# The last unit of an RWKV time-mixing kernel: both V projections ahead of the previous unit's output matmuls, copies and stores shared out anew

## The chip, the cores and the metric

The kernel runs on one core of a Trainium2 chip. The metric is the device time of one launch in microseconds (us); less is better. The kernel before takes 204.8 us (median of 5 runs, 204.01 to 205.72).

The engines are called PE (TensorE, matrix multiplies; PEld is its weight loading), DVE (VectorE), ACT (ScalarE), POOL (GpSimd) and SP (SyncE). SP does no arithmetic here: it issues DMAs. A DMA is issued by an instruction in the stream of SP, ACT or POOL, and 16 DMA engines then move its packets. Matrix products are written to PSUM; from there ACT or DVE copies them to on-chip memory (SBUF), and a DMA stores them to the output in device memory (HBM).

## The reference

`x` has shape (16, 2048, 256) in float32, and `x_prev` is `x` shifted by one row along the sequence.

```
xv = x * time_mix_v + x_prev * (1 - time_mix_v)
xr = x * time_mix_r + x_prev * (1 - time_mix_r)
v = xv @ value_weight
r = xr @ receptance_weight
out = (sigmoid(r) * v) @ output_weight        # float32, (16, 2048, 256)
```

The key projection is computed by the reference, but its result is not used, and the kernel leaves it out.

## The kernel before, in words

The 32,768 rows are worked in 64 **units** of 512 rows, numbered 0 to 63; four units make one batch. For each unit the kernel transposes its rows (by PE in the early batches, by DMA in the last four), mixes them with the previous rows, and then does, in bf16:

- R, the receptance projection (`project(..., 0)`, line 275, matmuls at L279) into PSUM, and a sigmoid on ACT (L513) into `s_sb`;
- V, the value projection (L279), and on DVE the product `z = s * v` (L548) into `z_sb`;
- O, the output projection (`out_matmuls`, line 301, matmuls at L303), a copy of the result from PSUM into `o_sb` in float32, and a store.

The order on every engine is the order in which the Python code records the instructions (`tc.manual_schedule()`); there is no planner. The framework adds the semaphore waits that the data and the reuse of buffers ask for. PSUM is full: `ps_t` has two buffers of one bank, and `ps_v`, `ps_r` and `ps_o` have one buffer of two banks each. A tile that is taken again from a pool of one buffer waits until its last reader is done.

The steady loop (lines 500 to 561) runs units 0 to 62. In the last rounds O of unit g-1 is recorded after V of unit g. From unit 60 on, `output` (line 323) does O in two halves of 256 rows by `out_part` (line 315): the matmuls, one copy, one store each. The stores before the last unit are all issued by SP.

The last unit, 63, is written out by hand in `last_unit` (line 347). It works in halves and quarters so that the end of the pipeline is short:

- line 358: R of half 0 into `psum_r` and its sigmoid (L360), R of half 1 into a `ps_t` buffer and its sigmoid;
- `value(h)` (line 361): V of half h, into `psum_v` for h = 0 and into the other `ps_t` buffer for h = 1, and the product z on DVE (L364);
- `before(h)` (line 368): half h of O of unit 62, whose z is `z_prev`: four matmuls (L303) into `psum_o` for h = 0 or `psum_r` for h = 1, a copy (L320) and a 256 KB store (L313);
- four quarters of O of unit 63 (lines 376 to 379): two matmuls each, into `psum_v`, `psum_o` and the two `ps_t` buffers; a 128x256 copy; a 128 KB store each.

In what follows, V63a and V63b are the two halves of V of unit 63, z63a and z63b their products on DVE, O62a and O62b the two halves of O of unit 62, and O63-0 to O63-3 the four quarters of O of unit 63. S62a, S62b and S63-0 to S63-3 are the stores of these six results, 1 MB together.

At the very end SP executes nine waits, one after the other, each on two semaphores: the lanes that count the landing of the DMAs. The framework deals each DMA one of 8 hardware lanes (SP and ACT) or one of 8 software lanes (POOL) and writes the nine waits in a fixed order. A barrier of all engines follows.

Of the kernel before, what the change touches and what calls it, by code (L numbers as in the profile page):

```python
# [15 lines left out]
def kernel(  # L16
# [25 lines left out]
    nc = tc.nc  # L42
# [11 lines left out]
    H = UJ // 2  # L54
# [16 lines left out]
    ps_t_pool = ctx.enter_context(tc.tile_pool(name="ps_t", bufs=2, space=bass.MemoryType.PSUM))  # L71
    ps_v_pool = ctx.enter_context(tc.tile_pool(name="ps_v", bufs=1, space=bass.MemoryType.PSUM))
    ps_r_pool = ctx.enter_context(tc.tile_pool(name="ps_r", bufs=1, space=bass.MemoryType.PSUM))
    ps_o_pool = ctx.enter_context(tc.tile_pool(name="ps_o", bufs=1, space=bass.MemoryType.PSUM))
# [200 lines left out]
    def project(ps, g, m, lo=0, hi=TU):  # L275
        b, e = divmod(g, UB)
        for mo in range(KO):
            for ko in range(KO):
                nc.tensor.matmul(  # L279
                    out=ps[:, mo, :],  # L280
                    lhsT=w_bf[:, m, ko, mo * P : (mo + 1) * P],
                    rhs=mixed((b, m, e * TU + lo, e * TU + hi))[:, :, ko],
                    start=(ko == 0),
                    stop=(ko == KO - 1),
                )
# [15 lines left out]
    def out_matmuls(ps, z, jj, slot):  # L301
        for ko in range(KO):
            nc.tensor.matmul(  # L303
                out=ps[:, slot, :],
                lhsT=z[:, ko, jj * P : (jj + 1) * P],
                rhs=wo_bf[:, ko, :],
                start=(ko == 0),
                stop=(ko == KO - 1),
            )

    def store(queue, b, lo, hi):
        dst = out[b].rearrange("(p j) d -> p j d", p=P)
        queue.dma_start(out=dst[:, lo:hi, :], in_=o_sb[b][:, lo:hi, :])  # L313

    def out_part(pool, name, z, b, e, jj, n, copy, queue):
        ps = pool.tile([P, n, D], FP32, name=name)
        for k in range(n):
            out_matmuls(ps, z, jj + k, k)
        lo = e * UJ + jj
        copy(out=o_sb[b][:, lo : lo + n, :], in_=ps)  # L320
        store(queue, b, lo, lo + n)
# [25 lines left out]
    def last_unit(g):  # L347


        b, e = divmod(g, UB)  # L350
        s_sb = zpool.tile([P, KO, TU], BF16, name="s_sb")
        z_sb = zpool.tile([P, KO, TU], BF16, name="z_sb")
        cols = [(h * H * P, (h + 1) * H * P) for h in range(2)]
        spare = [(ps_r_pool, "psum_r"), (ps_t_pool, "ps_t"), (ps_v_pool, "psum_v"), (ps_t_pool, "ps_t")]
        banks = [pool.tile([P, KO, H * P], FP32, name=name) for pool, name in spare]

        by_act, by_dve = nc.scalar.copy, nc.vector.tensor_copy
        for h, (lo, hi) in enumerate(cols):
            project(banks[h], g, 0, lo, hi)
            nc.scalar.activation(out=s_sb[:, :, lo:hi], in_=banks[h], func=ACT.Sigmoid)  # L360
        def value(h):
            lo, hi = cols[h]
            project(banks[2 + h], g, 1, lo, hi)
            nc.vector.tensor_tensor(  # L364
                out=z_sb[:, :, lo:hi], in0=s_sb[:, :, lo:hi], in1=banks[2 + h], op=ALU.mult
            )

        def before(h):
            pool, name = [(ps_o_pool, "psum_o"), (ps_r_pool, "psum_r")][h]
            out_part(pool, name, z_prev, b, e - 1, h * H, H, by_act, nc.sync)  # L370

        before(0)
        value(0)
        before(1)
        value(1)
        out_part(ps_v_pool, "psum_v", z_sb, b, e, 0, 1, by_act, nc.sync)
        out_part(ps_o_pool, "psum_o", z_sb, b, e, 1, 1, by_dve, nc.sync)
        out_part(ps_t_pool, "ps_t", z_sb, b, e, 2, 1, by_act, nc.scalar)
        out_part(ps_t_pool, "ps_t", z_sb, b, e, 3, 1, by_dve, nc.sync)

    def tile_for(b):

# [80 lines left out]
    by_act = {g: [] for g in range(-1, NU)}  # L463
# [36 lines left out]
    for g in range(NU - 1):  # L500
# [46 lines left out]
        z_sb = zpool.tile([P, KO, TU], BF16, name="z_sb")  # L547
# [9 lines left out]
        if shifted is not None and g == max(UB * (shifted - 2), CROSS + 2):  # L557
            nc.sync.dma_start(
                out=xt[shifted][:, 0, :, 1:P], in_=xt[shifted][:, J, :, 0 : P - 1]
            )  # L560
        z_prev2, z_prev = z_prev, z_sb
    last_unit(NU - 1)


# [28 lines left out]
```

## Time and profile before

| quantity | value |
|---|---|
| median of 5 runs | 204.8 us |
| the profiled execution, its own time | 205.07 us |
| its span, first to last instruction | 203.1 us |
| granted PE clock | 1.00 |
| busy share: PE / DVE / ACT / POOL | 97% / 92% / 88% / 41% |
| DMA, mean over the span | 281 GB/s |
| last matmul of O62b / of O63-3 ends | 197.55 us / 199.45 us |
| last copy (S63-3's data) ends | 199.90 us |
| last store issued by SP | 199.93 us |

The span is 1.9 us shorter than the execution's own time; what lies around it belongs to starting and ending a launch. Over the whole kernel PE is the busy engine. The change touches only what happens after about 196 us, where PE runs out of work, so the end has to be read by itself: on a timeline of the last 8 us, which gives for each instruction its start, its length and the wait before it, and in windows that show how much of the time the 16 DMA engines were busy.

### The profile page before, as it was taken

To read this page: it belongs to the slowest core of one execution; us is meant where nothing else is said; L and a number is where in the kernel's file an instruction comes from. 1 tells how busy PE (TensorE), PEld (TensorE's weight loads), DVE (VectorE), ACT (ScalarE), POOL (GpSimd) and SP (SyncE) were. 2 spreads that over 40 slices of the span, in tenths; PEclk is the share of its full clock that TensorE was granted. 3 is DMA by queue.
4 is the path that set the end of the run, shared out by engine and by line. 5 is a ranking of instruction groups with operands and counts; after the bars stand their busy time and mean duration, and the time that the engine had idled before them with its cause. 6 is when DMAs were issued, how large, how long until landed. Compare 5 with 4: busy or idle time off the path is not lost.

```text
span 203.1 us, 3923 instructions
## 1 busy us (share of the span) xinstructions
PE 196.6 (97%) x1436; PEld 127.4 (63%) x1436; DVE 186.7 (92%) x301; ACT 179.3 (88%) x198; POOL 83.3 (41%) x109
## 2 busy tenths in 40 slices
PE   7999999999999999999999999999999999999992
PEld 6766566666666666666666666656565656665571
DVE  3589999999999999999999999999999999999962
ACT  2399999999999999999999999998899999999981
POOL 1744462354344625426443444423444444444200
PEclk9999999999999999999999999999999999999999
DMA  4999999999999999999999999989999999999475
GB/s 164 295 155 216 215 280 275 277 282 271 290 315 307 319 309 300 311 305 289 296 294 290 312 302 290 323 292 205 295 175 359 249 341 254 259 418 377 203 305 207
DMA packets 32186, 57.00 MB, mean 281 GB/s; under 512 B 20772, under 2 KB 22056, under 8 KB 29096
## 3 DMA queue, kind: packets, MB, share of 16 engines
q1 hardware_dynamic: 27216, 40.50, 59.1%
q0 software_dynamic: 4800, 16.12, 40.0%
q8 instruction: 11, 0.18, 0.3%
q10 hardware_dynamic: 152, 0.13, 0.2%
q14 instruction: 7, 0.06, 0.1%
HBM read 34.34 MB, written 33.55 MB: 334 GB/s over the span
## 4 chain that ended last, share of the span: by engine, by line
PE 87%; ACT 4%; DVE 2%; issue 2%; DMA 2%; SPq 0%; DVEq 0%; ACTq 0%
PE psum_v L279 25%; PE psum_o L303 25%; PE psum_r L279 25%; PE ps_t L200 9%; DMA o_sb<-in_x_dram 2%; ACT s_sb L513 2%; PE psum_r L293 1%; ACT o_sb L335 1%; DVE mix L271 1%; DVE z_sb L548 1%; PE psum_v L223 1%; PE ps_t L144 1%; PE ps_t L303 1%; DVE mix L249 1%; ACT mix L491 1%
## 5 line engine op out<-in xcount | busy, mean ns | idle before, releaser
L259 POOL TENSOR_SCALAR mix<-xt,c_sb 128x1024 bf16<-128x1024 bf16 (+1 forms) x55 | 61.0, 1109 | 91.6 <-DVE mix L271 83.8
L548 DVE TENSOR_TENSOR z_sb<-s_sb,psum_v 128x1024 bf16<-128x1024 bf16 x63 | 76.7, 1217 | 3.4 <-PE psum_v L279 1.7
L271 DVE TENSOR_TENSOR mix<-mix,xt 128x1024 bf16<-128x1024 bf16 x112 | 77.2, 697 | 1.7
L279 PEld LDWEIGHTS <-w_bf 128*128 128x128 bf16 x516 | 48.6, 98 | 38.5 <-issue 1.1
L513 ACT ACTIVATE s_sb<-psum_r 128x1024 bf16<-128x1024 f32 x63 | 65.0, 1032 | 5.1 <-PE psum_r L279 4.8
L335 ACT COPY o_sb<-psum_o 128x1024 f32<-128x1024 f32 x60 | 61.1, 1018 | 7.1 <-PE psum_o L303 7.1
L279 PE MATMUL psum_v<-mix,w_bf 128*128 128x512 bf16 (+1 forms) x256 | 65.3, 378 | 0.4 <-DVE z_sb L548 0.2
L279 PE MATMUL psum_r<-mix,w_bf 128*128 128x512 bf16 (+1 forms) x252 | 64.3, 378 | 0.3 <-ACT s_sb L513 0.3
L303 PE MATMUL psum_o<-wo_bf,z_sb 128*128 128x256 bf16 x494 | 64.4, 273 | 0.1
L303 PEld LDWEIGHTS <-z_sb 128*128 128x128 bf16 x512 | 49.9, 98 | 20.1 <-DVE z_sb L364 0.8
L216 ACT COPY xt<-ps_t 128x1024 bf16<-128x1024 bf16 x38 | 38.7, 1029 | 0.0
L200 PEld LDWEIGHTS <-x_bf 128*128 128x128 bf16 x344 | 22.6, 98 | 9.2
L200 PE MATMUL ps_t<-ident,x_bf 128*128 128x128 bf16 x344 | 25.8, 219 | 0.0
L249 DVE TENSOR_SCALAR mix<-xt,c_sb 128x1024 bf16<-128x1024 bf16 (+1 forms) x50 | 22.5, 459 | 0.0
L491 ACT ACTIVATE mix<-xt,c_sb 128x1024 bf16<-128x1024 bf16 x11 | 12.8, 1159 | 0.0
L109 POOL DMA_DIRECT2D x_bf<-in_x_dram x14 | 10.5, 753 | 0.0
L271 DVE TENSOR_TENSOR mix<-mix,xt_first 128x1024 bf16<-128x1024 bf16 x15 | 10.2, 685 | 0.1
L259 POOL TENSOR_SCALAR mix<-xt_first,c_sb 128x512 bf16<-128x512 bf16 x6 | 4.1, 685 | 9.6 <-DVE xt_first L408 8.0
L249 DVE TENSOR_SCALAR mix<-xt_first,c_sb 128x512 bf16<-128x512 bf16 x22 | 6.8, 358 | 0.3
L216 ACT COPY xt_first<-ps_t 128x1024 bf16<-128x1024 bf16 x5 | 5.2, 1034 | 0.0
L144 PE MATMUL ps_t<-zeros 128*128 128x128 bf16 x31 | 3.7, 313 | 1.0 <-DVE zeros L87 1.0
L209 ACT CAST xt_first<-ps_t 128x512 bf16<-128x512 f32 x4 | 2.1, 588 | 2.3 <-PE ps_t L200 2.3
(63 smaller groups left out, 49.1 us busy)
## 6 DMA issues: line engine op xcount, KB each, us to landing
out_dram<-o_sb SPq DMA_DIRECT2D x28, 1024.0 KB, 9.8
x_bf<-in_x_dram POOLq DMA_DIRECT2D x14, 1024.0 KB, 25.3
out_dram<-o_sb SPq DMA_DIRECT2D x4, 512.0 KB, 3.7
out_dram<-o_sb SPq DMA_DIRECT2D x6, 256.0 KB, 2.1
x_bf<-in_x_dram POOLq DMA_DIRECT2D x5, 256.0 KB, 7.2
o_sb<-in_x_dram SPq DMA_DIRECT2D x2, 512.0 KB, 4.9
o_sb<-in_x_dram SPq DMA_DIRECT2D x2, 256.0 KB, 3.4
out_dram<-o_sb SPq DMA_DIRECT2D x3, 128.0 KB, 1.9
```

The costliest lines, as they stand in the source:

```text
L109: return nc.gpsimd.dma_start(out=x_bf[b], in_=rows(b), max_dma_last_dim=8192)
L200: nc.tensor.transpose(out=ps[:, jj], in_=src[:, jj, ko * P : (ko + 1) * P], identity=idn)
L216: nc.scalar.copy(out=xt[b][:, j0 : j0 + UJ], in_=ps)
L249: nc.vector.tensor_scalar(out=mixed(piece)[:, :, ko], in0=xt[b][:, slots(piece), ko], scalar1=c_sb[:, m, ko : ko + 1], scalar2=None, op0=A ...
L259: op = nc.gpsimd.tensor_scalar(out=mixed(piece)[:, :, 1], in0=xt[b][:, slots(piece), 1], scalar1=c_sb[:, m, 1:2], scalar2=1.0, op0=ALU.mul ...
L271: return nc.vector.tensor_tensor(out=mixed(piece), in0=mixed(piece), in1=xt[b][:, slots(piece, 1)], op=ALU.add)
L279: nc.tensor.matmul(out=ps[:, mo, :], lhsT=w_bf[:, m, ko, mo * P : (mo + 1) * P], rhs=mixed((b, m, e * TU + lo, e * TU + hi))[:, :, ko], st ...
L303: nc.tensor.matmul(out=ps[:, slot, :], lhsT=z[:, ko, jj * P : (jj + 1) * P], rhs=wo_bf[:, ko, :], start=(ko == 0), stop=(ko == KO - 1),)
L335: nc.scalar.copy(out=o_sb[b][:, j0 : j0 + UJ, :], in_=ps)
L491: nc.scalar.activation(out=mixed(piece)[:, :, ko], in_=xt[b][:, slots(piece), ko], func=ACT.Copy, scale=c_sb[:, m, ko : ko + 1],)
L513: nc.scalar.activation(out=s_sb, in_=ps_r, func=ACT.Sigmoid)
L548: nc.vector.tensor_tensor(out=z_sb, in0=s_sb, in1=ps_v, op=ALU.mult)
```

## The change

Only `last_unit` changes. The two halves of V of unit 63 are recorded ahead of both halves of O of unit 62; before, they alternated, O62a, V63a, O62b, V63b. The copy of O62b goes from ACT to DVE and its store from SP's queue to POOL's. The quarters of unit 63 exchange their copying engines and queues:

| result | copied by, before | after | stored by, before | after |
|---|---|---|---|---|
| O62a | ACT | ACT | SP | SP |
| O62b | ACT | DVE | SP | POOL |
| O63-0 | ACT | ACT | SP | SP |
| O63-1 | DVE | ACT | SP | SP |
| O63-2 | ACT | DVE | ACT | SP |
| O63-3 | DVE | ACT | SP | ACT |

No matmul, copy or byte is added or taken away, and PSUM buffers stay as they were.

```diff
         def before(h):
             pool, name = [(ps_o_pool, "psum_o"), (ps_r_pool, "psum_r")][h]
-            out_part(pool, name, z_prev, b, e - 1, h * H, H, by_act, nc.sync)
-
+            copy, queue = [(by_act, nc.sync), (by_dve, nc.gpsimd)][h]
+            out_part(pool, name, z_prev, b, e - 1, h * H, H, copy, queue)
+
+        value(0)
+        value(1)
         before(0)
-        value(0)
         before(1)
-        value(1)
         out_part(ps_v_pool, "psum_v", z_sb, b, e, 0, 1, by_act, nc.sync)
-        out_part(ps_o_pool, "psum_o", z_sb, b, e, 1, 1, by_dve, nc.sync)
-        out_part(ps_t_pool, "ps_t", z_sb, b, e, 2, 1, by_act, nc.scalar)
-        out_part(ps_t_pool, "ps_t", z_sb, b, e, 3, 1, by_dve, nc.sync)
+        out_part(ps_o_pool, "psum_o", z_sb, b, e, 1, 1, by_act, nc.sync)
+        out_part(ps_t_pool, "ps_t", z_sb, b, e, 2, 1, by_dve, nc.sync)
+        out_part(ps_t_pool, "ps_t", z_sb, b, e, 3, 1, by_act, nc.scalar)
```

In the built program the six stores of units 62 and 63 are waited for by SP's nine last waits in these places: before, S63-2 in the third, S63-3 in the fourth; after, S62b (POOL's lane) and S63-2 in the third, S63-3 in the ninth.

## The prediction

> **What bounds the kernel now.** The page's chain of waits is 87% PE over the whole span, but the change acts only after 196 us, so I read the end in four views: the timeline, the DMA windows, the transfer rows, and the waits that close the program.
>
> The timeline (start, length, what ran, wait before it and its releaser) gives the chain of the last copies:
>
> ```profile
> 196.08 0.60 PE L303 MATMUL psum_o<-wo_bf,z_sb 128*128 128x256 bf16 x4
> 196.51 0.60 PE L279 MATMUL psum_v<-mix,w_bf 128*128 128x256 bf16 x4
> 196.88 0.62 ACT L320 COPY o_sb<-psum_o 128x512 f32<-128x512 f32 x1
> ...
> 197.22 0.69 DVE L364 TENSOR_TENSOR z_sb<-s_sb,psum_v 128x512 bf16<-128x512 bf16 x1 [1.29 <-PE psum_v L279]
> ...
> 198.09 0.69 DVE L364 TENSOR_TENSOR z_sb<-s_sb,ps_t 128x512 bf16<-128x512 bf16 x1 [0.18 <-PE ps_t L279]
> ...
> 198.70 0.42 DVE L320 COPY o_sb<-psum_o 128x256 f32<-128x256 f32 x1
> ...
> 198.84 0.61 PE L303 MATMUL ps_t<-wo_bf,z_sb 128*128 128x256 bf16 x4 [0.26 <-DVE z_sb L364]
> 199.26 0.37 ACT L320 COPY o_sb<-ps_t 128x256 f32<-128x256 f32 x1 [0.50 <-PE ps_t L303]
> 199.48 0.42 DVE L320 COPY o_sb<-ps_t 128x256 f32<-128x256 f32 x1 [0.37 <-PE ps_t L303]
> ```
>
> V63b ends late, z63b follows at 198.09, and PE stands until 198.84 for the last two quarters. This wait is what the change attacks. But the windows tell of a second bound. Columns: window, length, five engines' busy time, clock, busy share of the 16 DMA engines, GB/s:
>
> ```profile
> 197.90:198.35 0.45, 0.45 (x5) 0.31 (x4) 0.27 (x2) 0.27 (x1) 0.00 (x0) 1.00 0.00 0
> 198.36:201.31 2.95, 0.82 (x6) 0.31 (x4) 1.18 (x3) 0.74 (x2) 0.00 (x0) 1.00 0.97 349
> 201.47:203.10 1.63, 0.00 (x0) 0.00 (x0) 0.00 (x0) 0.00 (x0) 0.00 (x0) 1.00 0.00 0
> ```
>
> The DMA engines are idle until 198.36, then 97% busy for 2.95 us with the 1 MB of the six last stores. The first to be issued is S62a, by SP at 197.52; its packets move 0.84 us later. So the end is set by when this stretch starts and how long 1 MB takes, more than by the last copy. The last store, issued at 199.93, moves its last packet at 201.47.
>
> Then SP's closing waits (their number, lengths in ns, starts):
>
> ```profile
> L588 SPq EVENT_SEMAPHORE  x1: 28/28/28, 201.6 to 201.6; - x1
> ...
> L588 SPq EVENT_SEMAPHORE  x2: 27/28/28, 201.9 to 202.0; - x2
> ```
>
> The wait for S63-3, fourth of nine, ends at 201.94; five more follow 0.06 us apart, then a barrier, and the span ends at 203.15, 1.21 us after that wait.
>
> **The change, part by part.** Times are after's, worked out from before's rows. Four matmuls take 0.44 us from start to start; a copy or product starts 0.70 us after the first of the four matmuls it reads (V63a at 196.51, z63a at 197.22), 0.43 us after the first of two (O63-0 at 197.96, its copy at 198.39).
>
> *V63a and V63b first.* V63a starts at 196.08 instead of 196.51, V63b at 196.51 instead of 197.38. `psum_v` must be free of the product of unit 62 (L548, 194.71 + 1.22 = 195.93): it is, by 0.15 us, so this wait costs nothing; were the product later, PE and all behind it would be late by the excess. z63a runs at 196.78, and z63b, no longer waiting for PE but for DVE itself (0.61 us from one product to the next), at 197.40 to 198.08. Gain: z63b 0.69 us earlier.
>
> *O62a and O62b later.* O62a starts at 196.95 (+0.87), O62b at 197.38 (+0.43). O62a's copy on ACT runs 197.58 to 198.20 instead of to 197.50, so S62a is issued at 198.23 instead of 197.52: **+0.71 us**. Nothing hides it: the DMA engines are idle by then.
>
> *Added wait.* O63-1 reuses `psum_o` and must wait for that copy: ready at 198.04 after O63-0 at 197.82, it starts at 198.25, so 0.21 us lost. Behind it on PE stand O63-2 and O63-3, at 198.47 and 198.69 instead of 198.84 and 199.06.
>
> *Copies.* The 128x512 DVE copy of O62b has no row. 0.42 us for 256 columns and 0.69 for a product of 512 give 0.69; one that costs ACT's 0.59 or twice the 256 row, 0.84, bounds it. It runs 198.02 to 198.71, before O63-2 is ready at 198.89, so even 0.84 is hidden. The others: ACT O63-0 198.24 to 198.61, ACT O63-1 198.67 to 199.04, DVE O63-2 198.89 to 199.31, ACT O63-3 199.11 to 199.48.
>
> *Stores issued*, before and after: S62a 197.52, 198.23; S62b 198.19, 198.74 (POOL); S63-0 198.79, 198.64; S63-1 199.22, 199.07; S63-2 199.67, 199.44 (SP is free of S63-1 only at 199.40); S63-3 199.93, 199.52. The last issue comes **0.42 us earlier**. Taken alone, that is the gain.
>
> *The DMA engines.* The same 1 MB now starts at 198.23 + 0.84 = 199.07, not 198.36. No store is ready before S62a, and all but POOL's are ready when the one ahead ends: a 256 KB store occupies the engines for some 0.7 us, a 128 KB one for some 0.4 (2 x 0.7 + 4 x 0.4 = 3.0, the stretch). So the stretch ends 0.71 us later, less at most the 3% that it stood idle before (0.09): **+0.62 to +0.71 us**. The 0.42 us is swallowed.
>
> *POOL's store.* POOL has been idle since 190.6 and holds only the end behind it. The trace has no store from POOL. Its nearest row is a 256 KB load: issued at 6.75, no software packet before 8.4, landed 5.3 us after issue beside other loads. At 198.74 that gives first packets at 200.4. The SP and ACT stores need 0.7 + 4 x 0.4 = 2.3 us, to 201.4, so POOL's packets fall into a full stretch and need not lengthen it: I take 0. Below: if POOL's packets moved beside the others, 0.67 us would leave the stretch. Above: if it landed 5.3 us after issue, at 204.0, the waits and barrier would end near 205.3, 1.5 us above the forecast.
>
> The Trainium skill ("DMA: Bandwidth & Descriptors", section "Issuing engines are not separate DMA queues") speaks against the sharing out: all issuers end in the same 16 engines, and several issuers save only issue time. No row here shows a store from POOL next to SP's; by that rule the lower bound falls away and the stretch stays full. The same page ("Latency and other measured facts") gives about 0.6 us to the first byte for SP and ACT and 1 us for POOL; the trace has 0.84 and 1.7, and by the page's difference of 0.4 S62b would still fall inside the stretch, so the sum would stay.
>
> *Closing waits.* The store that ends the stretch is then S62b or S63-2, both in the third wait, one place earlier than S63-3 before: one more wait after it, +0.06. Should S63-3, now in the ninth, land last, five fewer follow: -0.30.
>
> **Sum**: +0.62 to +0.71, and +0.06: about **+0.7 us** on the profiled span, 203.15 to 203.85; +0.3 if S63-3 lands last. The profiled execution took 205.07, 0.27 above the median; I put the difference on the median: 204.8 + 0.7 = **205.5**, in itself 205.0 to 205.8. That is +0.34%, within 0.5%, about what a measurement of this kernel can tell from no change (1.02 us).
>
> **Rivals.**
>
> *A, the forecast*, the full DMA stretch starts later: 205.5. For it: 97%, and zero before it. Chance 0.62.
>
> *B, POOL's store is the last to land: slower.* Place: S62b, third wait. It decides as soon as POOL's packets come after 201.4, 2.6 us after issue, or take longer. Price: over the page's queue rows POOL's queue needs 40.0% of the engines for 16.12 MB, SP's 59.1% for 40.50, so 1.7 times the time for a written byte; 0.7 us becomes 1.2, on top of A +0.5: 206.0. By the 5.3 us row 207.0. For it: no packet of POOL's first load for 1.7 us. Against: those loads change the type, reading two bytes for each written, and were beside other loads. Chance 0.26, taken at 206.3.
>
> *C, the chain of copies sets the end: faster.* If the DMA engines take three queues at a higher rate than one, or the stretch still has slack, the 0.42 us comes through, with the ninth wait -0.72 in all: 204.1 to 204.8, taken at 204.4. Against: 349 GB/s at 97%. Chance 0.12.
>
> That the order isn't as written is excluded: the built program has it. The one step that could undo it is the wait on `psum_v`, with 0.15 us to spare.
>
> **Numbers.** The likeliest is A, 205.5. The range reaches down to C's middle, 204.4, and up to 206.6, B's first price and some half of its way to the second; some 0.06 and 0.10 lie outside. Faster by over 0.5% (below 203.8) needs more than C's far end: 0.03. Slower (above 205.8): all of B and a little of A, 0.30. Within: 0.67.
>
> **What would show it.** In the profile after: z63b near 197.4; S62a issued near 198.2 and the DMA engines idle from 197.9 to about 199.1; then a stretch of some 3 us at 95% or more; last copy near 199.5, earlier than before, and yet a later end. B shows as software packets after 201.4, C as a stretch well under 2.8 us or with idle time in it. I am wrong if S62a moves less than 0.4 us, or if 1 MB takes less than 2.5 us.

## The result and the profile after

The changed kernel takes 205.35 us (median of 54 runs), the kernel before 204.48 us (median of 94 runs beside them). The ratio is 1.004, 95% interval 1.0028 to 1.0052: slower by about 0.8 us, or 0.4%. The profiled execution took 205.54 us with a span of 203.6 us.

Up to unit 63 both programs are the same, yet its first R matmul started at 195.19 us in the profile before and at 194.89 after. In all the profiles below that start lies between 193.8 and 195.8, so spans and single times scatter by more than the effect. The measure used from here on is the **tail**, from that matmul to the end of the span, worked out from the trace: 7.96 us before, 8.74 after, **+0.78**. One kernel profiled twice (the sixth experiment) gave tails of 7.65 and 7.66. Subtract 0.30 from a predicted time to find it in this timeline of after (start, length, engine, line, what):

```profile
195.76 0.60 PE L279 MATMUL psum_v<-mix,w_bf 128*128 128x256 bf16 x4
...
196.64 0.60 PE L303 MATMUL psum_o<-wo_bf,z_sb 128*128 128x256 bf16 x4
...
197.07 0.68 DVE L364 TENSOR_TENSOR z_sb<-s_sb,ps_t 128x512 bf16<-128x512 bf16 x1
197.27 0.59 ACT L320 COPY o_sb<-psum_o 128x512 f32<-128x512 f32 x1 [0.56 <-PE psum_o L303]
...
197.71 0.69 DVE L320 COPY o_sb<-psum_r 128x512 f32<-128x512 f32 x1
197.91 0.38 PE L303 MATMUL psum_o<-wo_bf,z_sb 128*128 128x256 bf16 x2
...
198.13 0.60 PE L303 MATMUL ps_t<-wo_bf,z_sb 128*128 128x256 bf16 x4
...
198.54 0.42 DVE L320 COPY o_sb<-ps_t 128x256 f32<-128x256 f32 x1
198.70 0.61 POOL L313 DMA_DIRECT2D out_dram<-o_sb  x1 [8.45 <-DVE o_sb L320]
198.76 0.37 ACT L320 COPY o_sb<-ps_t 128x256 f32<-128x256 f32 x1
199.16 0.40 ACTq L313 DMA_DIRECT2D out_dram<-o_sb  x1
```

PE no longer waits for z63b (197.07 to 197.75; the quarters that need it start at 198.13), and the last copies end near 199.1, relative to the start of unit 63 about half a microsecond earlier than before. But O62a's copy, 197.27, is later, and S62a is issued only at 197.89. The DMA windows show what that does (length, engines' busy time, clock, DMA share, GB/s):

```profile
197.62:198.71 1.09, 1.07 (x9) 0.58 (x6) 0.95 (x3) 0.98 (x3) 0.01 (x1) 1.00 0.00 0
...
198.72:201.89 3.17, 0.01 (x1) 0.00 (x0) 0.25 (x1) 0.37 (x1) 0.59 (x1) 1.00 0.92 331
```

In the kernel before the idle time ahead of the last stores was 0.45 us; now it is 1.1. The stretch itself, first packet to last, is hardly longer: the same window of before is

```profile
198.36:201.47 3.11, 0.82 (x6) 0.31 (x4) 1.18 (x3) 0.74 (x2) 0.00 (x0) 1.00 0.93 337
```

So the 1 MB was moved nearly as fast as before (331 against 337 GB/s, 0.05 us more), and began 0.66 us later. The transfer rows of after, for two stores issued between 198.6 and 199.2 (last column: us from issue to landing), show the stores queueing. ACT's 128 KB store took 3.1 us:

```profile
out_dram<-o_sb POOLq DMA_DIRECT2D x1, 256.0 KB, 3.1
out_dram<-o_sb ACTq DMA_DIRECT2D x1, 128.0 KB, 3.1
```

ACT's 128 KB store of before took 1.9:

```profile
out_dram<-o_sb ACTq DMA_DIRECT2D x1, 128.0 KB, 1.9
```

SP's closing waits of after, from the third on:

```profile
L589 SPq EVENT_SEMAPHORE  x7: 28/28/28, 202.4 to 202.8; - x7
```

The third of nine ends at 202.4 with the landing of S63-2; the other six follow at 0.06 us each.

### The profile page after: what moved, and what is told of

Same layout as the page of the kernel before. It is cut to its first block, busy times and chain, and to the rows that moved or that the text cites. A ratio compares the mean times of both kernels' runs of the same rounds, so it can differ in the third digit from the quotient of the medians.

```text
span 203.6 us, 3922 instructions
## 1 busy us (share of the span) xinstructions
PE 195.9 (96%) x1436; PEld 127.4 (63%) x1436; DVE 187.5 (92%) x301; ACT 179.2 (88%) x198; POOL 84.4 (41%) x110
## 4 chain that ended last, share of the span: by engine, by line
PE 80%; issue 7%; DVE 6%; ACT 2%; DMA 1%; POOL 1%; POOLq 0%; ACTq 0%; DVEq 0%
PE psum_v L279 23%; PE psum_o L303 22%; PE psum_r L279 22%; PE ps_t L200 9%; DVE z_sb L549 3%; DVE mix L271 2%; DMA tm_rows<-in_time_mix_v_dram 1%; PE psum_r L293 1%; DVE mix L249 1%; ACT s_sb L514 1%; POOL mix L259 1%; PE ps_t L144 1%; ACT o_sb L335 1%; PE psum_r L223 1%; ACT xt L216 0%
## 5 line engine op out<-in xcount | busy, mean ns | idle before, releaser
L249 DVE TENSOR_SCALAR mix<-xt,c_sb 128x1024 bf16<-128x1024 bf16 (+1 forms) x50 | 23.3, 475 | 0.0
L313 POOL DMA_DIRECT2D out_dram<-o_sb x1 | 0.6, 611 | 8.4 <-DVE o_sb L320 8.4
```

Of the source, the lines that this page charges most:

```text
L249: nc.vector.tensor_scalar(out=mixed(piece)[:, :, ko], in0=xt[b][:, slots(piece), ko], scalar1=c_sb[:, m, ko : ko + 1], scalar2=None, op0=A ...
```

## The experiments

Times in this table are us behind the first R matmul of unit 63, from the traces. "Busy for good" is when the DMA engines start the run that they do not leave until the last packet; "place" is the closing wait, of nine, that the last store to land stands in.

| kernel | S62a issued | last issue | busy for good | left to move | last packet | place | tail | ratio to before, 95% interval |
|---|---|---|---|---|---|---|---|---|
| before | 2.33 | 4.75 | 3.17 | 1 MB | 6.28 | 4 | 7.96 | |
| after | 3.00 | 4.38 | 3.83 | 1 MB | 6.99 | 3 | 8.74 | 1.004 (1.0028 to 1.0052) |
| x1_order | 3.00 | 4.90 | 3.83 | 1 MB | 6.89 | 4 | 8.56 | 1.0055 (1.0029 to 1.0081) |
| x2_share | 2.33 | 5.02 | 4.43 | 768 KB | 6.94 | 3 | 8.65 | 1.0066 (1.0035 to 1.0097) |
| x3_sp | 3.00 | 4.95 | 3.83 | 1 MB | 6.88 | 4 | 8.57 | 1.0024 (0.9996 to 1.0053) |
| x4_after_bare | none | 4.33 | 4.27 | 512 KB | 6.09 | 2 | 7.82 | 0.9987 (0.9965 to 1.0009) |
| x5_before_bare | none | 4.75 | 4.44 | 512 KB | 6.29 | 2 | 8.03 | 0.9986 (0.9966 to 1.0007) |
| x6_lanes | 2.33 | 4.75 | 3.17 | 1 MB | 6.28 | 9 | 7.65 | 0.998 (0.9949 to 1.0011) |
| x6_lanes_again | 2.33 | 4.75 | 3.16 | 1 MB | 6.29 | 9 | 7.66 | 0.998 (0.9955 to 1.0004) |
| x7_mid | 2.33 | 4.84 | 4.27 | 768 KB | 6.64 | 4 | 8.31 | 1.0007 (0.9989 to 1.0025) |

The theory on trial, T, is the prediction's: the DMA engines get the same bytes later. Its first rival, P, came from the profile after: POOL's store takes turns with S63-2 and S63-3, and perhaps that alone stretched their landing.

A second rival, that the end follows the last issue, can be read off the table. Before, the last packet came 1.53 us behind the last issue. That interval would put the last packet of after at 5.91, where it came at 6.99, and those of x1, x2, x3 and x7 between 6.37 and 6.55, where they came at 6.64 to 6.94. In these four the last issue is later than before, but that explains at most 0.27 us.

**x1_order: the new order alone.** The edit, against the changed kernel, takes back everything else:

```diff
-            copy, queue = [(by_act, nc.sync), (by_dve, nc.gpsimd)][h]
-            out_part(pool, name, z_prev, b, e - 1, h * H, H, copy, queue)
+            out_part(pool, name, z_prev, b, e - 1, h * H, H, by_act, nc.sync)
...
-        out_part(ps_o_pool, "psum_o", z_sb, b, e, 1, 1, by_act, nc.sync)
-        out_part(ps_t_pool, "ps_t", z_sb, b, e, 2, 1, by_dve, nc.sync)
-        out_part(ps_t_pool, "ps_t", z_sb, b, e, 3, 1, by_act, nc.scalar)
+        out_part(ps_o_pool, "psum_o", z_sb, b, e, 1, 1, by_dve, nc.sync)
+        out_part(ps_t_pool, "ps_t", z_sb, b, e, 2, 1, by_act, nc.scalar)
+        out_part(ps_t_pool, "ps_t", z_sb, b, e, 3, 1, by_dve, nc.sync)
```

> The changed kernel with only its new order (V63a and V63b ahead of O62a and O62b); copies and stores as before, nothing from POOL. The yardstick is the tail, from the first matmul of R of unit 63 to the end of the span: 7.96 us before, 8.74 after. Theory T (the DMA engines get the same 1 MB later because S62a is issued some 0.7 us later): tail 8.6 to 8.8, as after. Rival P (POOL's store, which in the profile after takes turns with S63-2 and S63-3 and stretches their landing from 1.9 to 3.1 us, is what costs): tail 7.5 to 8.0, no slower than before.

The tail is 8.56, a hair under T's 8.6 to 8.8 and 0.60 above before: the order carries most of the loss, without anything from POOL. P falls as the main cause.

**x3_sp: the changed kernel with S62b on SP.** Against the changed kernel:

```diff
-            copy, queue = [(by_act, nc.sync), (by_dve, nc.gpsimd)][h]
+            copy, queue = [(by_act, nc.sync), (by_dve, nc.sync)][h]
```

> The changed kernel with one word changed: S62b is issued by SP, not POOL. T: S62a starts the stretch as late as after and the bytes are the same, so tail 8.6 to 8.8. P: the cost goes with POOL's store, tail 7.9 to 8.2.

The tail is 8.57, far from P's 8.2, again just under T's band. Its windows have the same hole and the same load, with no POOL in them:

```profile
197.60:198.66 1.06, 1.04 (x9) 0.56 (x6) 0.92 (x3) 0.96 (x3) 0.00 (x0) 1.00 0.00 0
...
198.68:201.73 3.05, 0.00 (x1) 0.00 (x0) 0.25 (x1) 0.37 (x1) 0.00 (x0) 0.81 0.95 343
```

Against after the stretch is 0.1 us shorter, and the place of the last store in the closing waits is one later, worth 0.06: together the 0.17 us between the two tails. So P is true at most as a small term. It rests on one profile of each kernel, and the stretches without any POOL store run from 3.04 to 3.12 us themselves (x3, x6). The ratio's interval, 0.9996 to 1.0053, tells nothing of it.

**x2_share: the new copies and queues alone, in the order before.** The edit is the rest of the diff of the change, without its four lines of order.

> The kernel before with only the new copies and queues (O62b copied by DVE and stored by POOL, the quarters exchanged); its order of matmuls kept. T: S62a is issued as early as before, so the end is not moved by it; but O62b's copy (0.69) now stands ahead of z63b on DVE, z63b ends 0.5 later, and the last copies and stores with it: tail 8.4 to 8.6. P: as much or more, 8.5 to 9.0, with S62b landing last.

The tail is 8.65, 0.05 above T's band and inside P's. S62b is not the last to land (6.35 against 7.36 for S63-3), so P's mechanism, in that form, isn't it. What the windows show is a second hole, 0.4 us, between S62a and the next store, and later a dip:

```profile
198.94:199.76 0.82, 0.24 (x3) 0.03 (x2) 0.74 (x2) 0.65 (x2) 0.38 (x1) 1.00 0.81 317
199.77:200.18 0.41, 0.41 (x4) 0.27 (x4) 0.01 (x1) 0.00 (x0) 0.22 (x1) 1.00 0.00 0
...
200.55:200.77 0.22, 0.00 (x0) 0.00 (x0) 0.04 (x1) 0.20 (x1) 0.00 (x0) 1.00 0.34 103
```

S62b, issued at 3.61 instead of 3.01 and a further 1.4 us on its way from POOL, comes too late to follow S62a. The dip ends with the first packet of S62b, at 5.00. S63-1, issued by SP at 4.02, moves its own first packet only at 5.18, where in x5, issued at the same 4.02, it moves by 4.92; whether POOL's store holds it up, no run here tells. The dip is worth some 0.14 us: x7, with the same 768 KB and no such dip, needs 2.37 us for them, x2 2.51. The two halves of the change are each slower by themselves. Their losses (0.60 and 0.69) do not add to that of the whole (0.78); that both are the same bytes coming late is the reading of the windows, not a measurement of its own.

**x7_mid: is it the start of S62a, or the last hole?** Against the kernel before:

```diff
-        before(0)
-        value(0)
-        before(1)
-        value(1)
+        before(0)
+        value(0)
+        value(1)
+        before(1)
```

> The kernel before with the order O62a, V63a, V63b, O62b; copies and stores as before. S62a is issued as early as before (2.33 us behind the first matmul of R of unit 63), the last store 0.2 us earlier (4.55), but S62b comes 0.5 us later, and the DMA engines run dry behind S62a. T in the strict form (the end goes with the start of S62a): tail 7.9 to 8.0. T in the form that counts bytes (what is left to move when the DMA engines become busy for good; here 768 KB at about 4.3 us): tail 8.3 to 8.5.

The tail is 8.31, in the band of the form that counts bytes, though S62a is as early as before. The windows, with one hole ahead of S62a and one behind it:

```profile
196.53:196.94 0.41, 0.41 (x5) 0.31 (x4) 0.41 (x1) 0.32 (x1) 0.00 (x0) 1.00 0.00 0
196.96:197.78 0.82, 0.81 (x6) 0.31 (x4) 0.57 (x2) 0.71 (x3) 0.00 (x0) 1.00 0.81 317
197.80:198.04 0.24, 0.00 (x0) 0.00 (x0) 0.23 (x1) 0.16 (x1) 0.00 (x0) 1.00 0.00 0
198.06:200.43 2.37, 0.00 (x0) 0.00 (x0) 0.17 (x1) 0.00 (x0) 0.00 (x0) 0.85 0.93 332
```

It is the last hole that counts, with the bytes still behind it. T stands in that form. One expectation was missed: the last store was issued at 4.84, not 4.55, because SP's issues follow one another there; that is 0.09 us later than before and cannot make 0.35. (The time does not settle the 0.35 us of the tail, 0.17%: its interval, 0.9989 to 1.0025, holds both that and no change.)

**x4_after_bare and x5_before_bare: the stores S62a and S62b left out.** In both the call of `store` in `out_part` is skipped for unit 62, here as in x4:

```diff
-    def out_part(pool, name, z, b, e, jj, n, copy, queue):
+    def out_part(pool, name, z, b, e, jj, n, copy, queue, stored=True):
...
-        store(queue, b, lo, lo + n)
+        if stored:
+            store(queue, b, lo, lo + n)
...
-            out_part(pool, name, z_prev, b, e - 1, h * H, H, copy, queue)
+            out_part(pool, name, z_prev, b, e - 1, h * H, H, copy, queue, False)
```

> The changed kernel without the stores S62a and S62b (512 KB of the output are not written; everything is computed and copied). With half of the bytes gone the DMA engines should no longer bind, and the chain of copies sets the end. T: S63-0 to S63-3 are issued as early as after, the last at 4.4 us behind the first matmul of R of unit 63, and the tail falls from 8.74 to about 7.3, S63-3 being in the ninth wait. Rival C' (the new order itself is late, by a stall on PE, DVE or ACT, whatever the bytes): tail 8.4 or more.

> The kernel before without the stores S62a and S62b (512 KB of the output not written). T: before, its last stores are bound by their own issue almost as much as by the bytes, so it gains little: tail 7.9 to 8.0 with S63-3 in the second wait (7.96 with all stores). So with the bytes gone the new order is the better one by some 0.65 us, with them it is the worse by 0.78. Rival C': the bare changed kernel is slower than the bare kernel before.

x5 came out at 8.03, a hair above its band, and x4 at 7.82: the changed kernel is the better one once the bytes are gone, so the sign turns and C' (8.4) falls. This shows in the tails alone; the times (0.9987 and 0.9986) do not tell the two apart. The size, 0.21 and not 0.65, was a miss, and it lies in x4 (7.3 forecast). Most of it is the place: S63-2, not S63-3, landed last in x4, in the second wait and not the ninth, with seven more to follow at 0.06 us each. The last run of the DMA engines, in x4 and then in x5:

```profile
199.11:200.93 1.82, 0.00 (x0) 0.00 (x0) 0.00 (x0) 0.00 (x0) 0.00 (x0) 1.00 0.84 288
```

```profile
199.08:200.93 1.85, 0.00 (x0) 0.00 (x0) 0.28 (x1) 0.01 (x1) 0.00 (x0) 0.92 0.82 283
```

Four quarter stores take 1.8 us in either, and it is not a full stretch, because the DMA engines catch up with the issues. In x4 their share dips ahead of the second store:

```profile
199.48:199.64 0.16, 0.00 (x0) 0.00 (x0) 0.00 (x0) 0.00 (x0) 0.00 (x0) 1.00 0.46 148
```

In x5 it dips ahead of the second and of the third:

```profile
199.40:199.60 0.20, 0.00 (x0) 0.00 (x0) 0.00 (x0) 0.00 (x0) 0.00 (x0) 1.00 0.57 185
...
199.92:200.06 0.14, 0.00 (x0) 0.00 (x0) 0.00 (x0) 0.00 (x0) 0.00 (x0) 1.00 0.57 183
```

So even without S62a and S62b the end does not go with the last issue, which is 0.42 us earlier in x4, but with the third of the four. ACT issues it at 4.28 in x4 and at 4.48 in x5, its first packet moves at 5.19 and 5.38, and the last packet of all comes 0.90 us later in both. (In x4 the share ahead of this store falls only to 0.81, for 0.09 us, so the second store, issued at 3.86, binds there almost as much.)

The other lesson is x5 against before: half of the bytes gone, and the last packet at the same 6.29. In both, the first packet of S63-2 moves at 5.38, and before has a dip there too, though a smaller one:

```profile
200.48:200.68 0.20, 0.00 (x0) 0.00 (x0) 0.00 (x0) 0.00 (x0) 0.00 (x0) 1.00 0.81 272
```

Before the change the end was held twice, by S62a with 1 MB (3.17 + 3.11 = 6.28) and by S63-2 with 256 KB (5.38 + 0.90 = 6.28). After it, the first is late (3.83 + 3.16 = 6.99) and the second would allow 6.09, as in x4.

**x6_lanes: the place in the closing waits.** Five more stores, for units 54 to 59, shift the dealing of lanes so that S63-3 stands in the ninth wait; `last_unit` is that of before. Against the kernel before:

```diff
         elif g >= NU - 8:
-            store(nc.sync, b, j0, j0 + UJ)
+            store(nc.sync, b, j0, j0 + H)
+            store(nc.sync, b, j0 + H, j0 + UJ)
+        elif g == NU - 9:
+            store(nc.sync, b, j0 - UJ, j0)
+            store(nc.sync, b, j0, j0 + UJ)
```

> The kernel before with five more, smaller stores for units 54 to 59 (the 512 KB stores of units 56 to 59 in halves, the 1 MB store of units 54 and 55 in two), well ahead of the end; the last unit is untouched. The only aim is the place of S63-3 in SP's closing waits: ninth instead of fourth. If the closing waits count one by one as I read them, five waits of 0.06 us go from behind the landing: tail 7.66, 0.3 less. Rival: another thing (the barrier, a drain) ends last and the place is free of cost: tail 7.96.

> The same kernel as x6_lanes, the five more stores well ahead of the end, once more, because 0.3 us is hardly above the scatter of the times: tail 7.65 again, and a time 0.1 to 0.3% below the kernel before. If the first run's lower time came from elsewhere: tail 7.65 and no difference in time.

Tails 7.65 and 7.66 with the last packet at 6.28 and 6.29: as expected, the whole 0.3 us lies behind the landing. The closing wait of S63-3 (at 200.8) is now followed directly by the drains that lead to the barrier:

```profile
L592 SPq DRAIN  x2: 7/7/7, 200.9 to 200.9; - x2
L592 SPq EVENT_SEMAPHORE  x1: 28/28/28, 200.8 to 200.8; - x1
```

Both runs have a ratio of 0.998, each with an interval that takes in 1. It is the shortest tail of all whole kernels here; in the time it is a gain of about 0.2% that these runs do not settle.

## Why the prediction was right, and where it was not

The forecast was +0.7 us, by a DMA stretch that starts later; measured were +0.78 in the tail and +0.4% (0.28% to 0.52%, some 0.6 to 1.1 us) in the time. (The time itself, 205.35, lies below the forecast 205.5 although the change is a little larger than forecast: the forecast started from 204.8, and the kernel before now came out at 204.48.) The mechanism is the one forecast. Of the tail's +0.78, the later first packet makes 0.66 (forecast 0.71), the length of the stretch 0.05 (forecast nothing, or up to 0.09 less), and what follows the last packet 0.07 (forecast 0.06). The first came out smaller and the second larger, and the two errors partly cancel; that much of the agreement is luck. Step by step:

- *V first, z63b earlier*: forecast 197.40, less 0.30 is 197.10; it ran at 197.07. The wait on `psum_v` cost nothing: V63a followed R without a gap.
- *S62a later*: +0.71 forecast, +0.66 measured, for the reason given. The prediction let a copy start 0.70 us after the first of its four matmuls, but priced this one by the 0.63 of O62b's copy; 0.63 is what ran (196.64 to 197.27), and 0.70 would have made the forecast +0.78. x1 keeps the order alone, x3 all but POOL's store; both have this step and most of the loss.
- *Added wait on `psum_o`*: O63-1 at 197.91, 0.18 us late (0.21 forecast).
- *DVE copy of 128x512*: 0.69 forecast, 0.69 measured.
- *The last issue earlier*: S63-3 came 0.06 us sooner than forecast, but S63-2 0.13 later, at 199.27. It was issued 0.48 us behind S63-1, where 0.37 had been forecast: SP's issue of S63-1 took 0.39 us and not 0.33, and a wait of SP's stands between the two. S63-2 became the last to land.
- *POOL's store at no cost*: first packet 1.55 us after issue, well inside the stretch as forecast, but the stretch is 0.1 us longer than with S62b on SP. Rival B's mechanism, POOL's store landing last, did not happen: it landed at 201.80, 0.6 us before S63-2. The sign named for B did appear: POOL's packets run from 200.25 to 201.35, which is 201.65 in the prediction's times and past its 201.4. So that sign could not tell B from A.
- *A stretch of some 3 us at 95% or more*: 3.17 us at 92% from the first packet to the last; without its last 0.14 us it is 0.95.
- *Closing waits*: +0.06 forecast from fourth to third place; x6 shows the same rule at five places. The other case, 0.30 less with S63-3 the last to land, was priced too simply: S63-3 landed only 0.05 us before S63-2, and had it come just behind, the third wait and the six after it would still have held the end.

One reading was too simple. The prediction said of the kernel **before** that its end is set by the start of the stretch and its bytes "more than by the last copy", and it priced rival C by the 0.42 us of the last issue. x5 shows that before was held equally by the last two quarter stores, from the issue of S63-2 on, and x4 that the gain free of the bytes is 0.2 us. The sum came out right because the change made the first bound the later one by far, 6.99 against 6.09.

## What to carry to other kernels

In these runs the end of a kernel that stores until the last is the latest, over the stores, of "when this store can start moving" plus "the time of all bytes from it on"; an edit that brings the last store forward and an early, larger one back pays with the larger. Look for the last hole in the DMA share, a dip included, and at what is left behind it before counting the chain of the last copies. And measure such an edit between two marks in the trace: here the tail of one kernel came out the same within 0.01 us in two profiles, where the times of one kernel scatter by some two microseconds.

## What the runs showed of the hardware

- SP's closing waits are served one by one at 0.06 us, so the lane of the last store is worth some 0.4 us between the places seen: from the last landing to the end it took 1.34 us in the second place (x5), 1.27 in the third (after), 1.23 in the fourth (before) and 0.92 in the ninth (x6).
- POOL's 256 KB store was moved in 64 packets of 4 KB, where SP's moves 128 of 2 KB. From issue to the first packet it took 1.55 us, against 0.84 from SP.
- POOL's drain behind that store lasted 4.03 us and ended 0.2 us before SP reached the barrier. In a shorter tail it might have been the last; no run here tried that.

```profile
L589 POOLq DRAIN  x1: 4032/4032/4032, 198.7 to 198.7; - x1
```
